# A one-core fp32 trunk layer: the first three up weight sets loaded into raw buffers of their own and split some blocks later, and the second part of the output projection reordered with its first two blocks interleaved

## The chip, the cores and the metric

The kernel runs on one core of one Trainium2 chip. The metric is the device time of one execution in microseconds (us). Before the change it is 1489.62 us, the median of three runs (1489.47 to 1491.08). A core has five engines that run their own instruction queues in order: PE (TensorE, matrix products), DVE (VectorE), ACT (ScalarE), POOL (GpSimd) and SP (SyncE, which here issues the weight transfers). In the profile, PEld is the weight load of PE.

## The reference

One layer for 320 tokens (256 of a prompt, 64 of a running sample), width 2048, in fp32:

```python
h = rmsnorm(x, g_pre_mix);  p = h @ w_in
a = conformer_conv(...)     # 8 channel groups of 128: GLU, causal depthwise conv of width 31,
                            # per-token group norm, silu
b = gated_delta(...)        # 8 heads of 128
x = x + rmsnorm(concat(a, b) @ w_out, g_post_mix)
h = rmsnorm(x, g_pre_ffn);  gu = causal_dwconv(h @ w_up)        # width 3, 2 x 5632 columns
x = x + rmsnorm((silu(gate) * up) @ w_down, g_post_ffn)
```

Beside the new x, the states of the convolutions and of the delta rule are returned.

## The kernel before

**Products.** All activations lie feature-major, as 16 blocks of 128 features by T = 320 tokens. A fp32 product is made of three products in a rounded type, fp32r: each weight and each activation is split into hi (rounded) and lo (the rest), and hi·hi, hi·lo and lo·hi are summed in one PSUM bank. So every 128x128 piece of a weight costs three matmuls of 128x320. A weight comes in pieces of 128 x 640, 768 or 1024: `load_dma` (L204-210) has SP load it into a ring `wst` of three buffers; `split_w` has ACT cast it to hi (L217) and DVE subtract to lo (L218), into a ring `wsp` of three pairs. `load_split` does both, under `boost`, a priority that lets the scheduler put them earlier than where they are written. Activations are split likewise, by `split_act` (L241 on ACT, L242 on DVE).

**Order.** The kernel is written in Python, and a scheduler orders the instructions by priority and data; `tc.issue_after(i)` forbids it to put the instructions inside ahead of i. Side work of the conv and delta heads is cut into jobs (`advance`) and into `taps`, which are handed out every few matmuls (`tick`); `finish` and `finish_conv` write what is left.

**Conv blocks.** The conv of one of the eight channel groups is 32 taps on DVE (L560 to L563, in two accumulators, added by L557). `conv_tail` then goes PE transposes `pt_c` (L578), DVE statistics (L580, L581, L584, L585), POOL (L586, L587), ACT normalises (L591), PE transposes back (L595), ACT silu (L597), and the split into `bh7`, `bl7` (for group 7). Groups 6 and 7 are the last ones: their taps run beside the first part of the output projection.

**Output projection, two parts.** `KORDER` lists the 16 feature blocks of concat(a, b) in the order of use, and `bx(k)` gives the pair of block KORDER[k]. In the first part (L1004 to L1009) 15 of the 16 output blocks n sum over the first K1 = 11 entries of KORDER; each takes two weight pieces (6 and 5 wide, matmuls L233, L234, then L237). `while jobs: advance(jobs[0])` then writes the rest of the conv jobs. In the second part (L1046 to L1072) all 16 output blocks take the last five entries, 5, 6, 7 (conv) and 14, 15 (delta): one piece `w_out2` of 128x640 each, three matmuls (L1061, L1062, L1063) for each entry, then the evacuation: DVE adds to the first part (L1069), ACT squares (L1032), DVE sums the squares (L1034), ACT scales by g2 (L1072). SP also loads block n of x into x1 (L1050).

**The up group.** A norm follows (`rstd`, `rstd_rows`, and `keep_warm`, L280, dummy matmuls), and a loop over the 16 feature blocks k on DVE and ACT: L1093 and L1094 (DVE, x1 + m·rb1), L1098 (ACT, hi2) and L1099 (DVE, lo2). `up_group` (L1108 to L1118) computes the first four output blocks of the up projection in four PSUM banks at once, k by k: 192 matmuls of L1117. Its weights are eight sets, each 128 x 4 x 256 of `w_up` (width 1024, two k's of four blocks), `upw[0]` to `upw[7]`. Two of them are loaded and split at n = 4 and 8 of the second part, through the ring `wst`, into a pool `ug` of two pairs; the six others in the norm loop, at k = 1, 3, ... 11, into the ring `wsp`. After that come the rest of the up projection and the down projection, which have no line in the diff.

Of the kernel before, what the change touches and what calls it, by code (L numbers as in the profile page):

```python
# [9 lines left out]
F32 = mybir.dt.float32  # L10
# [7 lines left out]
P = 128  # L18
D = 2048
KB = D // P  # L20
TP = 256
TS = 64
T = TP + TS
# [5 lines left out]
HALF = 1024  # L29
# [42 lines left out]
FIRST_V = 32  # L72
NFIRST = len(FIRST)
FW = NFIRST * P
KORDER = (0, 1, 2, 3, 4, 8, 9, 10, 11, 12, 13, 5, 6, 7, 14, 15)

S_ = 4

# [22 lines left out]
def trunk_kernel(ctx, tc, ins, outs):  # L101
    nc = tc.nc
    V, S, G, PE = nc.vector, nc.scalar, nc.gpsimd, nc.tensor
    PRI_W = 600
    boost = [0]
# [20 lines left out]
    def advance(job, behind=None):  # L126
        with tc.issue_after(behind or dense[0]), tc.high_priority(offset=PRI_J):
            try:
                wait, job[2], job[3], *kind = next(job[1])
                job[0] = dense[1] + wait  # L130
                job[4] = kind
            except StopIteration:
                jobs.remove(job)
        return next(i for i in reversed(nc.cur_bb.bb.instructions) if i.engine == dense[0].engine)
# [10 lines left out]
    def newest(engine, n0):  # L145
        return next((i for i in reversed(nc.cur_bb.bb.instructions[n0:]) if i.engine == engine), None)
# [32 lines left out]
    wst = ctx.enter_context(tc.tile_pool(name="wst", bufs=3))  # L179
# [3 lines left out]
    ps_p = ctx.enter_context(tc.tile_pool(name="ps_p", bufs=2, space=PSUM))  # L183
    ps_t = ctx.enter_context(tc.tile_pool(name="ps_t", bufs=2, space=PSUM))
# [7 lines left out]
    def pv(name, a=None, b=None):  # L192
        o, w = PAR[name]
        if a is None:
            return par[:, o:o + w]
        return par[:, o + a:o + (a + 1 if b is None else b)]
# [5 lines left out]
    pre = []  # L202
    ready = {}

    def load_dma(src):
        w = wst.tile([P, HALF], F32, tag="w", name="w")
        dst = w[:, 0:src.free_size()]
        if len(src.shape) == 3:
            dst = dst.rearrange("p (a f) -> p a f", a=src.shape[1])
        nc.sync.dma_start(dst, src)  # L210
        return w

    def split_w(w, width, pool=None):
        pool = pool or wsp
        hi = pool.tile([P, HALF], F32R, tag="whi", name="whi")
        lo = pool.tile([P, HALF], F32R, tag="wlo", name="wlo")
        S.copy(hi[:, 0:width], w[:, 0:width])  # L217
        V.tensor_tensor(lo[:, 0:width], w[:, 0:width], hi[:, 0:width].bitcast(F32), ALU.subtract)  # L218
        return hi, lo

    def load_split(src, width, pool=None):
        with tc.high_priority(offset=boost[0]):
            return split_w(load_dma(src), width, pool)

    def block_matmul(ps, src, rhs, nks, final=True, first=True):
        nk = sum(nks)
        k0 = 0
        for nk_part in nks:
            hi, lo = load_split(src[:, k0 * P:(k0 + nk_part) * P], nk_part * P)
            for j in range(nk_part):  # L230
                xh, xl = rhs(k0 + j)
                wh = hi[:, j * P:(j + 1) * P]
                tick(PE.matmul(ps, wh, xh, start=(first and k0 + j == 0), stop=False))  # L233
                tick(PE.matmul(ps, wh, xl, start=False, stop=False))  # L234
            for j in range(nk_part):
                xh, xl = rhs(k0 + j)
                tick(PE.matmul(ps, lo[:, j * P:(j + 1) * P], xh, start=False, stop=(final and k0 + j == nk - 1)))  # L237
            k0 += nk_part
# [77 lines left out]
    with tc.tile_pool(name="xp", bufs=1) as xp:  # L316
# [25 lines left out]
        with tc.high_priority(offset=PRI_E):  # L342
            keep_warm(psw, NWARM)

            last = {}
# [22 lines left out]
            for k in range(KB):  # L368
                x = xt[k // 4][:, k % 4, :]
# [15 lines left out]
        for i, b in enumerate(FIRST):  # L385
            pool = (ps_t, ps_g)[i // 2]
            ready[b] = pool.tile([P, 512], F32, tag=pool.name[-1], name="ps_first")
        for k0 in range(0, KB, 2):
            hi, lo = pre[k0 // 2]
            for ks in ((k0,), (k0 + 1,)) if k0 < 4 else ((k0, k0 + 1),):  # L390
                for wt in (hi, lo):
                    for k in ks:
                        for i, b in enumerate(FIRST):
                            ps = ready[b][:, 0:T]
                            o = (k - k0) * FW + i * P
                            w = wt[:, o:o + P]
                            xh, xl = hx(k)
# [606 lines left out]
    for n in range(KB - 1):  # L1004
        psm = ps_p.tile([P, 512], F32, tag="p", name="psm")
        block_matmul(psm[:, 0:T], ins["w_out1"][n], bx, (6, 5))
        m.append(act.tile([P, T], F32, tag=f"hl{n}", name=f"m{n}"))
        with tc.high_priority(offset=PRI_E):
            S.copy(m[n], psm[:, 0:T])  # L1009
    while jobs:  # L1010
        advance(jobs[0])
    pa.close()
    pb = ctx.enter_context(ExitStack())
    res = pb.enter_context(tc.tile_pool(name="res", bufs=1, reuse_waits="tile"))
    fb = pb.enter_context(tc.tile_pool(name="fb", bufs=2, reuse_waits="tile"))
    x1 = res.tile([P, KB, T], F32, tag="x1", name="x1")
# [17 lines left out]
            V.tensor_tensor(acc, acc, sq, ALU.add)  # L1034
        return sq

    ug = tc.tile_pool(name="ug", bufs=2, reuse_waits="tile")
    ugp = ug.__enter__()
    up_src = ins["w_up"][0:4].rearrange("a p f -> p a f")

    def up_weights(kk, pool=None):
        return load_split(up_src[:, :, kk * 256:(kk + 1) * 256], HALF, pool)

    upw = []
    nk2 = KB - K1
    for n in range(KB):  # L1046
        hi, lo = load_split(ins["w_out2"][n], nk2 * P)
        if n in (4, 8):
            upw.append(up_weights(len(upw), ugp))
        nc.sync.dma_start(x1[:, n:n + 1, :], ins["x"][:, n:n + 1, :])  # L1050
        if n == KB - 1:
            nc.sync.dma_start(fpar, ins["fpar"])
        whole = n == KB - 1
        pool = (ps_p, ps_t)[n // 2 % 2]
        psm = pool.tile([P, 512], F32, tag=pool.name[-1], name="psm2")
        if whole:
            block_matmul(psm[:, 0:T], ins["w_out1"][n], bx, (6, 5), False)
        for j in range(nk2):
            xh, xl = bx(K1 + j)
            o = j * P  # L1060
            PE.matmul(psm[:, 0:T], hi[:, o:o + P], xh, start=(j == 0 and not whole), stop=False)  # L1061
            PE.matmul(psm[:, 0:T], hi[:, o:o + P], xl, start=False, stop=False)  # L1062
            PE.matmul(psm[:, 0:T], lo[:, o:o + P], xh, start=False, stop=(j == nk2 - 1))  # L1063
        with tc.high_priority(offset=PRI_E):
            if whole:
                m.append(act.tile([P, T], F32, tag=f"hl{n}", name=f"m{n}"))
                src = psm[:, 0:T]
            else:
                V.tensor_tensor(m[n], m[n], psm[:, 0:T], ALU.add)  # L1069
                src = m[n]  # L1070
            last = square_acc(n, src)
            held = S.activation(m[n], src, AF.Identity, scale=pv("g2", n)).ins  # L1072
    boost[0] = 0
    rb2 = act.tile([P, T], F32, tag="rb", name="rb2")
    hi2, lo2 = [], []
    with tc.high_priority(offset=PRI_E):
        psw = ps_p.tile([P, 512], F32, tag="p", name="psw")
        rr, mm = rstd([acc, last])
        keep_warm(psw, 5, mm)
        rb1, mm = rstd_rows(rr)  # L1080
        keep_warm(psw, 10, mm)
        split = None
        for k in range(KB):
            if k % 2 == 1 and k < 13:
                with ExitStack() as e:
                    if k < 7:
                        e.enter_context(tc.issue_after(split))
                        e.enter_context(tc.issue_after(held))
                    upw.append(up_weights(len(upw)))
            with ExitStack() as e:  # L1090
                if 0 < k < 4:
                    e.enter_context(tc.issue_after(added))
                V.tensor_tensor(m[k], m[k], rb1, ALU.mult)  # L1093
            added = V.tensor_tensor(x1[:, k, :], x1[:, k, :], m[k], ALU.add).ins  # L1094
            g = pv("g3", k)
            hi2.append(act.tile([P, T], F32R, tag=f"hh{k}", name=f"hi2_{k}"))
            lo2.append(act.tile([P, T], F32R, tag=f"hl{k}", name=f"lo2_{k}"))
            S.activation(hi2[k], x1[:, k, :], AF.Identity, scale=g)  # L1098
            split = V.scalar_tensor_tensor(lo2[k], x1[:, k, :], g, hi2[k].bitcast(F32), ALU.mult, ALU.subtract).ins  # L1099
# [8 lines left out]
    def up_group():  # L1108
        pss = [ps_p.tile([P, 512], F32, tag="p", name="psu") for _ in range(2)]
        pss += [ps_t.tile([P, 512], F32, tag="t", name="psu") for _ in range(2)]  # L1110
        for k in range(KB):
            hi, lo = upw[k // 2]
            xh, xl = hx2(k)
            for n, (wt, x) in enumerate(((hi, xh), (lo, xh), (hi, xl))):
                for i in range(4):
                    o = i * 256 + k % 2 * P
                    PE.matmul(pss[i][:, 0:T], wt[:, o:o + P], x, start=(k == 0 and n == 0), stop=(k == KB - 1 and n == 2))  # L1117
        return {0: pss[0], NFB: pss[1], 1: pss[2], NFB + 1: pss[3]}  # L1118

    first = up_group()  # L1120
    ug.__exit__(None, None, None)
    yp = pb.enter_context(tc.tile_pool(name="yp", bufs=1, reuse_waits="tile"))
    y = yp.tile([P, KB, T], F32, tag="y", name="y")
# [200 lines left out]
```

## Time and profile before

| what | value |
|---|---|
| median of 3 runs | 1489.62 us (1489.47 to 1491.08) |
| the profiled execution | 1489.37 us, of which span 1487.6 us |
| granted TensorE clock | 1.00 in the mean |
| PE, PEld | 1478.6 us (99%), 1458.2 us (98%) |
| DVE, ACT, POOL | 996.6 us (67%), 730.8 us (49%), 230.5 us (15%) |
| DMA | 224.22 MB, mean 151 GB/s |

The page gives the profiled execution; its span starts with the first and ends with the last instruction, and 1.8 us of the execution lie outside. Times within the trace count from the start of the span. The first part of the output projection ends at about 490 us, the second part runs to 534 us, and the up group from 538.6 to 568.6 us. In a row of the timeline the columns are start, duration (of the whole group, where there is an xcount at the end), engine, line, operation, output<-input, shape, and in brackets the engine's idle time before it with what ended that. Where instructions of one kind follow each other on an engine, their starts lie closer together than their durations, since each begins before the one ahead has fully left; the difference of two starts is what one costs the queue.

### The profile page before, as it was taken

What the parts mean: (1) busy time and instruction counts of PE and PEld (TensorE: products, weight loads), DVE (VectorE), ACT (ScalarE), POOL (GpSimd) and SP (SyncE); (2) the same over time, 40 slices, a digit from 0 to 9 for tenths busy, and PEclk for the clock granted to TensorE, in tenths of its full rate; (3) what the DMA queues carried; (4) which work ended last, traced back from release to release, by engine and by line L of the source; (5) the groups of instructions that cost most, each with busy time, mean ns of one, the idle gap of its engine ahead of it and who ended that gap; (6) DMA issues with size and microseconds to landing.
All of it is one profiled execution on the core that took longest, in us unless ns stands there. A gap on an engine that the chain in (4) does not pass through costs nothing.

```text
span 1487.6 us, 27264 instructions
## 1 busy us (share of the span) xinstructions
PE 1478.6 (99%) x10610; PEld 1458.2 (98%) x10610; DVE 996.6 (67%) x1816; ACT 730.8 (49%) x1331; POOL 230.5 (15%) x390
## 2 busy tenths in 40 slices
PE   9999999999999999999999999999999999999998
PEld 8999999999999989999999999999999999999997
DVE  6779888888989678756336665545666545656554
ACT  7674556655454656544334444334444334444453
POOL 0111101021010000322002322002232001223101
PEclk9999999999999999999999999999999999999999
DMA  8435453544444734444554444554444455444453
GB/s 294 140 115 167 158 151 110 147 156 138 129 122 145 238 128 146 146 156 121 153 168 155 145 154 135 143 162 158 156 143 147 136 148 168 153 156 143 136 148 119
DMA packets 98281, 224.22 MB, mean 151 GB/s; under 512 B 18792, under 2 KB 39528, under 8 KB 98152
## 3 DMA queue, kind: packets, MB, share of 16 engines
q1 hardware_dynamic: 98008, 222.45, 47.8%
q8 instruction: 83, 1.36, 0.4%
q14 instruction: 46, 0.38, 0.1%
q10 hardware_dynamic: 144, 0.03, 0.0%
HBM read 215.33 MB, written 7.12 MB: 150 GB/s over the span
## 4 chain that ended last, share of the span: by engine, by line
PE 95%; ACT 2%; DVE 1%; issue 1%; DMA 0%; POOL 0%; DVEq 0%; ACTq 0%; POOLq 0%
PE psu L237 13%; PE psu L234 13%; PE psu L233 13%; PE psdn L233 7%; PE psdn L234 7%; PE psdn L237 7%; PE psq L233 3%; PE psq L234 3%; PE psq L237 3%; PE psm L237 2%; PE psm L233 2%; PE psm L234 2%; PE psu L1117 1%; PE psv L233 1%; PE psgate L233 1%; PE ps_first L398 1%
## 5 line engine op out<-in xcount | busy, mean ns | idle before, releaser
L217 ACT CAST whi<-w 128x1024 fp32r<-128x1024 f32 (+2 forms) x440 | 412.6, 940 | 488.5 <-PE psu L234 169.7
L218 DVE TENSOR_TENSOR wlo<-w,whi 128x1024 fp32r<-128x1024 f32 (+2 forms) x440 | 477.2, 1085 | 191.4 <-ACT whi L217 123.9
L233 PE MATMUL psu<-hi,whi 128*128 128x320 f32 x1344 | 397.0, 309 | 0.0
L234 PE MATMUL psu<-lo,whi 128*128 128x320 f32 x1344 | 396.9, 309 | 0.0
L234 PEld LDWEIGHTS psu<-lo,whi 128*128 128x128 f32 x1344 | 252.3, 188 | 0.0
L233 PEld LDWEIGHTS psu<-hi,whi 128*128 128x128 f32 x1344 | 252.2, 188 | 0.0
L237 PE MATMUL psu<-hi,wlo 128*128 128x320 f32 x1344 | 224.4, 309 | 0.0
L237 PEld LDWEIGHTS psu<-hi,wlo 128*128 128x128 f32 x1344 | 204.1, 188 | 0.0
L234 PE MATMUL psdn<-gl,whi 128*128 128x320 f32 x660 | 195.9, 310 | 0.0
L1150 POOL COPY nffn<-fbuf 128x2 f32<-128x2 f32 x88 | 99.5, 1131 | 586.7 <-DVE fbuf L1148 583.5
L1148 DVE TENSOR_TENSOR fbuf<-psu,rb 128x256 f32<-128x256 f32 x88 | 37.4, 424 | 169.1 <-PE psu L237 169.0
L233 PE MATMUL psdn<-gh,whi 128*128 128x320 f32 x480 | 142.8, 309 | 0.0
L234 PEld LDWEIGHTS psdn<-gl,whi 128*128 128x128 f32 x660 | 123.9, 188 | 0.3
L233 PE MATMUL psq<-hh,whi 128*128 128x320 f32 x352 | 106.0, 314 | 0.0
L234 PE MATMUL psq<-hl,whi 128*128 128x320 f32 x352 | 104.1, 309 | 0.0
L233 PEld LDWEIGHTS psdn<-gh,whi 128*128 128x128 f32 x480 | 90.1, 188 | 0.0
L237 PE MATMUL psdn<-gh,wlo 128*128 128x320 f32 x480 | 89.9, 309 | 0.0
L237 PEld LDWEIGHTS psdn<-gh,wlo 128*128 128x128 f32 x480 | 75.3, 188 | 0.0
L233 PEld LDWEIGHTS psq<-hh,whi 128*128 128x128 f32 x352 | 66.1, 188 | 0.4
L234 PEld LDWEIGHTS psq<-hl,whi 128*128 128x128 f32 x352 | 66.1, 188 | 0.2
L563 DVE SCALAR_TENSOR_TENSOR cvt<-ub,par,cvt 128x320 f32<-128x320 f32 x120 | 65.3, 545 | 0.1
L1193 DVE TENSOR_TENSOR y<-y,psdn 128x320 f32<-128x320 f32 x45 | 22.0, 488 | 58.7 <-PE psdn L237 58.7
(356 smaller groups left out, 2485.2 us busy)
## 6 DMA issues: line engine op xcount, KB each, us to landing
w<-in_w_up SPq DMA_DIRECT2D x176, 512.0 KB
w<-in_w_in SPq DMA_DIRECT2D x88, 512.0 KB
w<-in_w_down SPq DMA_DIRECT2D x64, 384.0 KB
w<-in_w_down SPq DMA_DIRECT2D x64, 320.0 KB
w<-in_w_out SPq DMA_DIRECT2D x32, 320.0 KB
w<-in_w_out SPq DMA_DIRECT2D x16, 384.0 KB
w<-in_w_first SPq DMA_DIRECT2D x6, 512.0 KB
wtp<-wsp SPq DMA_DIRECT2D x4, 640.0 KB
```

Of the source, the lines that this page charges most:

```text
L217: S.copy(hi[:, 0:width], w[:, 0:width])
L218: V.tensor_tensor(lo[:, 0:width], w[:, 0:width], hi[:, 0:width].bitcast(F32), ALU.subtract)
L233: tick(PE.matmul(ps, wh, xh, start=(first and k0 + j == 0), stop=False))
L234: tick(PE.matmul(ps, wh, xl, start=False, stop=False))
L237: tick(PE.matmul(ps, lo[:, j * P:(j + 1) * P], xh, start=False, stop=(final and k0 + j == nk - 1)))
L398: tick(PE.matmul(ps, w, xh, start=(k == 0 and wt is hi), stop=(k == KB - 1 and wt is lo)))
L563: return lambda: V.scalar_tensor_tensor(acc, x, w, acc, ALU.mult, ALU.add)
L1117: PE.matmul(pss[i][:, 0:T], wt[:, o:o + P], x, start=(k == 0 and n == 0), stop=(k == KB - 1 and n == 2))
L1148: V.tensor_tensor(buf[:, 2:258], psu[:, 0:TP], rb2[:, 0:TP], ALU.mult)
L1150: G.tensor_copy(nffn[:, b, 0, :], buf[:, 256:258])
L1193: V.tensor_tensor(y[:, n, :], y[:, n, :], psd[:, 0:T], ALU.add)
```

## The change

1. `KORDER` ends in 5, 14, 15, 6, 7 instead of 5, 6, 7, 14, 15, so in the second part the two delta blocks are used ahead of conv groups 6 and 7.
2. Blocks 0 and 1 of the second part are interleaved: four entries of block 0, four of block 1, then the last entry (conv 7) of block 0 and of block 1, and only then both evacuations.
3. `load_dma` can load into another pool. The first three up weight sets go into a pool `ur` of two raw buffers, loaded at n = 3, 6, 10 (`up_load`) and split at n = 6, 10, 14 (`up_split`) into `ug`, now three pairs. The norm loop makes five sets (k = 3, 5, ... 11).
4. The load and split of `w_out2` for n = 2 may not stand ahead of `flush`, the newest ACT instruction of the jobs' rest.

```diff
-KORDER = (0, 1, 2, 3, 4, 8, 9, 10, 11, 12, 13, 5, 6, 7, 14, 15)
+KORDER = (0, 1, 2, 3, 4, 8, 9, 10, 11, 12, 13, 5, 14, 15, 6, 7)
...
+    flush = len(nc.cur_bb.bb.instructions)
     while jobs:
         advance(jobs[0])
+    flush = newest(mybir.EngineType.Activation, flush)
...
-    ug = tc.tile_pool(name="ug", bufs=2, reuse_waits="tile")
+    ug = tc.tile_pool(name="ug", bufs=3, reuse_waits="tile")
     ugp = ug.__enter__()
+    ur = tc.tile_pool(name="ur", bufs=2, reuse_waits="tile")
+    urp = ur.__enter__()
     up_src = ins["w_up"][0:4].rearrange("a p f -> p a f")
-    def up_weights(kk, pool=None):
-        return load_split(up_src[:, :, kk * 256:(kk + 1) * 256], HALF, pool)
+    def up_load(kk, pool=None):
+        with tc.high_priority(offset=boost[0]):
+            return load_dma(up_src[:, :, kk * 256:(kk + 1) * 256], pool)
+    def up_split(w, pool=None):
+        with tc.high_priority(offset=boost[0]):
+            return split_w(w, HALF, pool)
...
     for n in range(KB):
-        hi, lo = load_split(ins["w_out2"][n], nk2 * P)
-        if n in (4, 8):
-            upw.append(up_weights(len(upw), ugp))
+        with ExitStack() as e:
+            if n == 2:
+                e.enter_context(tc.issue_after(flush))
+            w2 = load_split(ins["w_out2"][n], nk2 * P)
+        if n in (3, 6, 10):
+            upr.append(up_load(len(upr), urp))
+        if n in (6, 10, 14):
+            upw.append(up_split(upr[len(upw)], ugp))
...
+        if n == 0:
+            opened[0] = psm, w2
+            second(n, psm[:, 0:T], w2, range(nk2 - 1))
+            continue
+        if n == 1:
+            second(n, psm[:, 0:T], w2, range(nk2 - 1))
+            second(0, opened[0][0][:, 0:T], opened[0][1], (nk2 - 1,))
+            second(n, psm[:, 0:T], w2, (nk2 - 1,))
+        else:
+            second(n, psm[:, 0:T], w2, range(nk2))
...
-            if k % 2 == 1 and k < 13:
+            if k % 2 == 1 and 1 < k < 13:
...
-                    upw.append(up_weights(len(upw)))
+                    upw.append(up_split(up_load(len(upw))))
```

`second` holds the three matmuls and `evacuate` the evacuation, both as before.

What the scheduler makes of it is seen in the order of the instructions. In the rows below `w` is a raw weight piece, `whi` and `wlo` its parts, and a number behind a name tells tiles of one name apart.

On SP, in the first part of the output projection, before:

```order
L210 DMA w_5924<-in_w_out1 128x640
L210 DMA w_5956<-in_w_out1 128x768
L210 DMA w_5984<-in_w_out1 128x640
L210 DMA w_6012<-in_w_out1 128x768
L210 DMA w_6040<-in_w_out1 128x640
```

and after:

```order
L210 DMA w_5924<-in_w_out1 128x640
L210 DMA w_6406<-in_w_up 128x4x256
L210 DMA w_6492<-in_w_up 128x4x256
L210 DMA w_5956<-in_w_out1 128x768
L210 DMA w_5984<-in_w_out1 128x640
L210 DMA w_6610<-in_w_up 128x4x256
L210 DMA w_6012<-in_w_out1 128x768
```

The three loads of up sets stand in the first part, although they are written at n = 3, 6 and 10 of the second; there, none is left.

On DVE at the same place, where conv 6 gets its last sum (`cvt_4967`) and the taps of conv 7 (`cvt_5305`, `odd_5306`) begin, before:

```order
L218 TENSOR_TENSOR wlo_5903<-w_5900,whi_5902 128x768
L557 TENSOR_TENSOR cvt_4967<-cvt_4967,odd_4968 128x320
L563 SCALAR_TENSOR_TENSOR cvt_5305<-ub1_588,par_81,cvt_5305 128x320
L562 TENSOR_SCALAR odd_5306<-ub1_588,par_81 128x320
L563 SCALAR_TENSOR_TENSOR cvt_5305<-ub1_588,par_81,cvt_5305 128x320
L563 SCALAR_TENSOR_TENSOR odd_5306<-ub1_588,par_81,odd_5306 128x320
L218 TENSOR_TENSOR wlo_5927<-w_5924,whi_5926 128x640
L242 TENSOR_TENSOR bl5_5842<-af_5839,bh5_5841 128x320
```

and after:

```order
L218 TENSOR_TENSOR wlo_5903<-w_5900,whi_5902 128x768
L557 TENSOR_TENSOR cvt_4967<-cvt_4967,odd_4968 128x320
L218 TENSOR_TENSOR wlo_6495<-w_6406,whi_6494 128x1024
L218 TENSOR_TENSOR wlo_6613<-w_6492,whi_6612 128x1024
L218 TENSOR_TENSOR wlo_5927<-w_5924,whi_5926 128x640
L242 TENSOR_TENSOR bl5_5842<-af_5839,bh5_5841 128x320
L562 TENSOR_SCALAR odd_5306<-ub1_588,par_81 128x320
L563 SCALAR_TENSOR_TENSOR cvt_5305<-ub1_588,par_81,cvt_5305 128x320
L580 BN_STATS bst_5876<-pt_c_5875 128x6 x2
```

The splits of up sets 0 and 1 stand ahead of nearly all taps of conv 7; that of set 2 (`wlo_6729`) follows ten rows on, still ahead of most of them.

On DVE at the end of conv 7, before:

```order
L563 SCALAR_TENSOR_TENSOR cvt_5305<-ub1_588,par_81,cvt_5305 128x320
L218 TENSOR_TENSOR wlo_6152<-w_6149,whi_6151 128x640
L557 TENSOR_TENSOR cvt_5305<-cvt_5305,odd_5306 128x320
L242 TENSOR_TENSOR bl6_6107<-af_6104,bh6_6106 128x320
L218 TENSOR_TENSOR wlo_6194<-w_6191,whi_6193 128x768
L218 TENSOR_TENSOR wlo_6222<-w_6219,whi_6221 128x640
L580 BN_STATS bst_6166<-pt_c_6165 128x6 x2
```

and after:

```order
L242 TENSOR_TENSOR bl6_6107<-af_6104,bh6_6106 128x320
L563 SCALAR_TENSOR_TENSOR cvt_5305<-ub1_588,par_81,cvt_5305 128x320
L218 TENSOR_TENSOR wlo_6194<-w_6191,whi_6193 128x768
L563 SCALAR_TENSOR_TENSOR odd_5306<-ub1_588,par_81,odd_5306 128x320
L563 SCALAR_TENSOR_TENSOR cvt_5305<-ub1_588,par_81,cvt_5305 128x320
L563 SCALAR_TENSOR_TENSOR odd_5306<-ub1_588,par_81,odd_5306 128x320
L218 TENSOR_TENSOR wlo_6222<-w_6219,whi_6221 128x640
L563 SCALAR_TENSOR_TENSOR cvt_5305<-ub1_588,par_81,cvt_5305 128x320
L557 TENSOR_TENSOR cvt_5305<-cvt_5305,odd_5306 128x320
L580 BN_STATS bst_6166<-pt_c_6165 128x6 x2
```

The last sum of conv 7 (L557) stands behind `bl6_6107`, `wlo_6194` and `wlo_6222`, which stood behind it before. On PE the transposes that read it, before:

```order
L234 MATMUL psm_6124<-bl13_4881,whi_6151 128x320
L578 MATMUL pt_c_6165<-cst_82,cvt_5305 128x128 x3
L237 MATMUL psm_6124<-bp0_3030,wlo_6152 128x320
L237 MATMUL psm_6124<-bp1_3695,wlo_6152 128x320 x2
L237 MATMUL psm_6124<-bp2_4871,wlo_6152 128x320 x2
```

and after:

```order
L234 MATMUL psm_6124<-bl13_4881,whi_6151 128x320
L237 MATMUL psm_6124<-bp0_3030,wlo_6152 128x320
L237 MATMUL psm_6124<-bp1_3695,wlo_6152 128x320 x2
L237 MATMUL psm_6124<-bp2_4871,wlo_6152 128x320
L578 MATMUL pt_c_6165<-cst_82,cvt_5305 128x128 x3
L237 MATMUL psm_6124<-bp2_4871,wlo_6152 128x320
```

PE takes them four matmuls later in its own order than before. At the start of the second part, PE before takes conv 7 (`bh7`) behind nine matmuls, blocks 0 and 1 mixed by the scheduler; after, behind twelve of block 0 and twelve of block 1.

More of the change, by code (lines that the diff above doesn't have):

```diff
@@ L203, in trunk_kernel, with load_dma @@
     ready = {}
-    def load_dma(src):
-        w = wst.tile([P, HALF], F32, tag="w", name="w")
+    def load_dma(src, pool=None):
+        w = (pool or wst).tile([P, HALF], F32, tag="w", name="w")
         dst = w[:, 0:src.free_size()]
@@ L1035, in square_acc, with second, evacuate @@
         return sq
-    ug = tc.tile_pool(name="ug", bufs=2, reuse_waits="tile")
+    ug = tc.tile_pool(name="ug", bufs=3, reuse_waits="tile")
     ugp = ug.__enter__()
+    ur = tc.tile_pool(name="ur", bufs=2, reuse_waits="tile")
+    urp = ur.__enter__()
     up_src = ins["w_up"][0:4].rearrange("a p f -> p a f")
-    def up_weights(kk, pool=None):
-        return load_split(up_src[:, :, kk * 256:(kk + 1) * 256], HALF, pool)
-    upw = []
-    nk2 = KB - K1
-    for n in range(KB):
-        hi, lo = load_split(ins["w_out2"][n], nk2 * P)
-        if n in (4, 8):
-            upw.append(up_weights(len(upw), ugp))
[L1050 to L1058, printed above, removed]
+    def up_load(kk, pool=None):
[4 more added lines that the diff above has]
+            return split_w(w, HALF, pool)
+    upw, upr = [], []
+    nk2 = KB - K1
+    def second(n, psm, w, js):
+        hi, lo = w
+        for j in js:
             xh, xl = bx(K1 + j)
             o = j * P
-            PE.matmul(psm[:, 0:T], hi[:, o:o + P], xh, start=(j == 0 and not whole), stop=False)
-            PE.matmul(psm[:, 0:T], hi[:, o:o + P], xl, start=False, stop=False)
-            PE.matmul(psm[:, 0:T], lo[:, o:o + P], xh, start=False, stop=(j == nk2 - 1))
+            PE.matmul(psm, hi[:, o:o + P], xh, start=(j == 0 and n < KB - 1), stop=False)
+            PE.matmul(psm, hi[:, o:o + P], xl, start=False, stop=False)
+            PE.matmul(psm, lo[:, o:o + P], xh, start=False, stop=(j == nk2 - 1))
+    last = held = None
+    def evacuate(n, psm, whole):
+        nonlocal last, held
         with tc.high_priority(offset=PRI_E):
@@ L1072, in trunk_kernel @@
             held = S.activation(m[n], src, AF.Identity, scale=pv("g2", n)).ins
+    opened = {}
+    for n in range(KB):
+        with ExitStack() as e:
[6 more added lines that the diff above has]
+            upw.append(up_split(upr[len(upw)], ugp))
+        nc.sync.dma_start(x1[:, n:n + 1, :], ins["x"][:, n:n + 1, :])
+        if n == KB - 1:
+            nc.sync.dma_start(fpar, ins["fpar"])
+        whole = n == KB - 1
+        pool = (ps_p, ps_t)[n // 2 % 2]
+        psm = pool.tile([P, 512], F32, tag=pool.name[-1], name="psm2")
+        if whole:
+            block_matmul(psm[:, 0:T], ins["w_out1"][n], bx, (6, 5), False)
+        if n == 0:
[8 more added lines that the diff above has]
+            second(n, psm[:, 0:T], w2, range(nk2))
+        for n, psm in ((0, opened[0][0]), (1, psm)) if n == 1 else ((n, psm),):
+            evacuate(n, psm, whole)
     boost[0] = 0
@@ L1120, in trunk_kernel @@
     first = up_group()
+    ur.__exit__(None, None, None)
     ug.__exit__(None, None, None)
```

## The prediction

> **What bounds the kernel now.** I read the page first (engines, clock, the chain), then PE's list of waits, then a table of stretches around the change, and last the rows of each place.
>
> ```profile
> PE 1478.6 (99%) x10610; PEld 1458.2 (98%) x10610; DVE 996.6 (67%) x1816; ACT 730.8 (49%) x1331; POOL 230.5 (15%) x390
> PE 95%; ACT 2%; DVE 1%; issue 1%; DMA 0%; POOL 0%; DVEq 0%; ACTq 0%; POOLq 0%
> PE psm L1063 <- DVE wlo L218: 1.1, 2, 0.8
> core 0: us, PE busy (x) PEld busy (x) DVE busy (x) ACT busy (x) POOL busy (x), PEclk, DMA share, GB/s
> 452.00:478.00 26.00, 26.00 (x181) 25.97 (x181) 24.45 (x53) 12.25 (x22) 2.09 (x2) 1.00 0.46 137
> 494.00:511.00 17.00, 17.00 (x118) 16.90 (x116) 12.50 (x21) 13.19 (x23) 0.00 (x0) 1.00 0.88 287
> 511.00:515.00 4.00, 2.89 (x18) 2.45 (x17) 2.44 (x5) 1.83 (x4) 0.00 (x0) 1.00 0.80 231
> 538.60:568.60 30.00, 29.70 (x195) 28.43 (x194) 29.43 (x56) 15.24 (x25) 0.00 (x0) 1.00 0.38 122
> ```
>
> PE is busy for 99% of the span and is 95% of the chain that ended last: time falls only where PE stalls, and work moved to another engine costs only where PE comes to wait for it. The change adds and removes no matmul, cast or subtraction; it moves up splits. So I look for stalls that go and stalls that come. The stretches differ. In the first part (452 to 478) PE is full but DVE has only 1.55 us free in 26. In the second part DVE has 4.50 of 17 free, but the transfers are at 0.88 and 287 GB/s, and right behind PE loses time (511 to 515). In the up group DVE is full again, 29.43 of 30.
>
> **Part 1, the start of the second part (gain 0.31).**
>
> ```profile
> 491.76 0.31 PE L1063 MATMUL psm<-bh,wlo 128*128 128x320 f32 x1
> 492.81 0.31 PE L1063 MATMUL psm<-bh,wlo 128*128 128x320 f32 x1
> 510.86 0.31 PE L1062 MATMUL psm<-bl,whi 128*128 128x320 f32 x1
> 511.98 0.41 PE L1063 MATMUL psm<-bh,wlo 128*128 128x320 f32 x1 [0.81 <-DVE wlo L218]
> 512.23 0.31 PE L1061 MATMUL psm<-bh,whi 128*128 128x320 f32 x1
> 514.15 0.31 PE L1062 MATMUL psm<-bl,whi 128*128 128x320 f32 x1
> 514.76 0.42 PE L1063 MATMUL psm<-bh,wlo 128*128 128x320 f32 x1 [0.30 <-DVE wlo L218]
> 515.01 0.31 PE L1061 MATMUL psm<-bh,whi 128*128 128x320 f32 x1
> 539.56 0.75 PE L1117 MATMUL psu<-hi,wlo 128*128 128x320 f32 x4
> ```
>
> Unhindered, a matmul costs 0.147: in the last row four of them take 0.75, one 0.31, so three steps are 0.44. From 491.76 to 492.81 five starts take 1.05 instead of 0.73: 0.31 lost where conv 7 is first read. Now 24 matmuls, 3.5 us, stand ahead of that read instead of nine, 1.3; that is 2.2 more cover for a stall of 0.31. So it goes: 0.31 (bounds 0 and 0.31). The interleave itself costs nothing: the same matmuls, and two PSUM banks for blocks 0 and 1 as before.
>
> **Part 2, the jam in the middle of the second part (gain 1.65).** By the rows above, 510.86 to 512.23 is 1.37 for two steps worth 0.29, a loss of 1.08; 514.15 to 515.01 is 0.86, a loss of 0.57; together 1.65. What stands behind them:
>
> ```profile
> 508.48 1.73 ACT L217 CAST whi<-w 128x1024 fp32r<-128x1024 f32 x2 [1.70 <-DMA w<-in_w_up]
> 506.61 6.44 DMA w<-in_w_out
> w<-in_w_up SPq DMA_DIRECT2D x176, 512.0 KB
> ```
>
> ACT waited 1.70 for an up set, and the w_out piece for the second stall took 6.44 to land (the row of the chain). The change takes two loads of 512 KB, 1.05 MB, out of a stretch that moves 17 x 287 kB = 4.9 MB, and also two casts and two splits of 1024. Both stalls lose their cause, so I take all of 1.65; bounds 0 (the transfers stay late anyway) and 1.65.
>
> **Part 3, the up group (gain 1.1).**
>
> ```profile
> 538.61 1.12 PE L1117 MATMUL psu<-hi,whi 128*128 128x320 f32 x4
> 568.62 0.31 PE L234 MATMUL psu<-lo,whi 128*128 128x320 f32 x1
> 539.56 1.22 DVE L218 TENSOR_TENSOR wlo<-w,whi 128x1024 fp32r<-128x1024 f32 x1
> 540.69 0.54 DVE L1099 SCALAR_TENSOR_TENSOR lo<-x,par,hi 128x320 fp32r<-128x320 f32 x1
> ```
>
> 192 matmuls at 0.147 are 28.2; the group takes 568.62 - 538.61 = 30.01. Of the 1.8 over, up to 0.4 is three other matmuls in the stretch (195 against 192). The first 0.36 (538.61 to 539.56, 0.95 for four matmuls instead of 0.59) comes ahead of any split and stays. So 1.05 to 1.45 can go. DVE is full here, so PE goes at its pace, and one split fewer (five, not six) takes 540.69 - 539.56 = 1.13 out of its queue. I take 1.1; bounds 0 (the last splits, not their sum, set the end) and 1.45.
>
> **Part 4, what the moved splits hold up (cost 3.25).** By the order, the three up splits now run on DVE in the first part, ahead of the taps of conv 7.
>
> ```profile
> 453.04 0.48 DVE L557 TENSOR_TENSOR cvt<-cvt,odd 128x320 f32<-128x320 f32 x1
> 464.29 0.96 DVE L218 TENSOR_TENSOR wlo<-w,whi 128x768 fp32r<-128x768 f32 x1 [1.55 <-ACT whi L217]
> 477.44 0.49 DVE L557 TENSOR_TENSOR cvt<-cvt,odd 128x320 f32<-128x320 f32 x1
> 477.84 0.49 DVE L242 TENSOR_TENSOR bl<-af,bh 128x320 fp32r<-128x320 f32 x1
> 478.24 1.69 DVE L218 TENSOR_TENSOR wlo<-w,whi 128x768 fp32r<-128x768 f32 x2
> 479.51 0.49 PE L578 MATMUL pt_c<-cst,cvt 128*128 128x128 f32 x3
> 479.76 0.98 PE L237 MATMUL psm<-bp,wlo 128*128 128x320 f32 x5
> 462.37 1.16 ACT L591 ACTIVATE un<-pt_c,gnm,grs 128x128 f32<-128x128 f32 x3 [3.98 <-POOL gnm L587]
> ```
>
> Conv 7's last sum (L557) began at 477.44 and ended at 477.93; PE took its transposes (L578) at 479.51, so 1.6 us of slack. Now three splits of 1.14 stand ahead, 3.42 us, and by the order also `bl6` (0.40, 477.84 to 478.24) and two w_out splits (1.60 of the 1.69 row, less the overlap): 2.00. L557 begins at 477.44 + 5.42 = 482.86 and ends at 483.35. PE's turn comes four matmuls later than before, 479.51 + 0.59 = 480.10. PE stands for 483.35 - 480.10 = 3.25 us, with everything behind it in its queue: the fifth L237, then blocks n of the first part.
>
> Can DVE's idle 1.55 ahead of 464.29 take some of it up? It waits there for a cast behind conv 6's `un` (462.37), which waits for POOL, which waits for DVE's statistics. Those are pushed less than the taps: six taps that stood ahead of them now stand behind. But the rows between statistics and that cast are the same four taps and one split, so the idle time moves along and is not used: 0 taken up, 1.55 at most. The casts can wait for their loads:
>
> ```profile
> 445.20 2.58 SPq L210 DMA_DIRECT2D w<-in_w_out  x2
> 452.22 0.73 ACT L217 CAST whi<-w 128x640 fp32r<-128x640 f32 x1 [1.33 <-issue]
> 458.35 0.31 PE L233 MATMUL psm<-bp,whi 128*128 128x320 f32 x1
> ```
>
> The up loads are issued behind the second of these, at 447.78. 1.05 MB at 287 GB/s land at 451.4, at 137 GB/s at 455.4; with a cast of 0.87 set 1 is ready at 452.3 or 456.3, and DVE wants it at 453.52 + 1.14 = 454.66. So 0 to 1.6 more; I take 0, since the queue's load (0.46) leaves room. Bounds of the term: 1.7 and 4.9. The w_out cast at 452.22, first read by PE at 458.35, comes behind two up casts (1.74): with set 1 as late as 455.4 it ends at 455.4 + 0.87 + 0.73 = 457.0, still ahead of its reader, so nothing there. The slots for casts cost nothing else: ACT is free for 13.75 of 26. SP's later w_out loads stand behind three more issues; what times them is the ring of three buffers, that is the pace of the splits, not SP.
>
> The `flush` rule holds one w_out2 load until the jobs' last ACT work is placed; two pieces for blocks 0 and 1 (24 matmuls) cover it, so nothing.
>
> **Sum.** -0.31 - 1.65 - 1.1 + 3.25 = +0.19 on this execution's 1489.37, that is 1489.6. The median is 0.25 above that execution: 1489.8. I say 1489.7. With every bound the kind way (-0.31 - 1.65 - 1.45 + 1.7) it is 1.7 faster, the other way 4.9 slower.
>
> **The clock, row and rule.** A pause of 3.1 us (3.25 less the 0.16 for which the matmul ahead still runs) is longer than any that this trace has (its longest wait inside is 0.81), and a new question is whether the granted clock, 1.00 throughout, holds.
>
> ```profile
> 1.42 3.59 PE L280 MATMUL psw<-wz 128*128 128x512 bf16 x8 [1.42 <-POOL wz L250]
> 5.54 0.47 PE L398 MATMUL ps_first<-hh,whi 128*128 128x320 f32 x1
> 5.81 0.47 PE L400 MATMUL ps_first<-hl,whi 128*128 128x320 f32 x1
> 6.82 0.31 PE L400 MATMUL ps_first<-hl,whi 128*128 128x320 f32 x1
> ```
>
> After the start PE runs at 0.27 a matmul (5.54 to 5.81, each 0.47 long) and at 6.82 has the 0.31 of all later ones: 5.4 us from 1.42 at 0.147 / 0.27 = 0.55 of the pace, a loss of 2.4. That is what a drop would cost. The Trainium skill, "TensorE: Matmul & The Clock Gate", section "Why this matters for your kernels", asks for no PE-idle gaps over about 3 us, since one idle window halves the clock, and its Part 1 gives a free-running window of about 3.4 us. By it a pause of 3.1 lies at the limit and is an estimate away from it on either side: under it the sum stays 1489.7, over it 2.4 come on top. No run here shows it, and its limit is in none of the sums here.
>
> **Rivals.**
> - Clock drop (slower). Up set 1 lands 1.6 late (137 GB/s), PE stands 4.9 instead of 3.25, and the clock falls: 1489.7 + 1.6 + 2.4 = 1493.7. It decides if a drop comes at all, from some pause between 0.81 and 4.9; a shorter pause with a drop gives 1492.1. For it: the start shows that the clock is low after standing. Against: transfers have room.
> - Late landing without a drop: 1491.3.
> - The jam stays: x1 and w_out2 alone still fill the queue, part 2 brings nothing, 1491.3. Against: 4.9 - 1.05 = 3.9 MB in 17 us is 226 GB/s, under the 287 that were reached.
> - Conv 7 isn't late (the change does only what it says): the idle 1.55 and more is used up, or the splits wait aside; parts 1 to 3 alone, -3.06, 1486.6.
>
> **Chances.** A measurement of this kernel can tell about 0.2%, 2.98 us: below 1486.6 is faster, above 1492.6 slower. My forecast 0.63 (its own range, with some idle time used or half a us of late landing, 1488.2 to 1491.0); jam 0.09; late landing 0.08; clock drop 0.11; conv 7 not late 0.09. Faster: most of the last, 0.08. Slower: most of the drop and a little of late landing with the jam, 0.12. Same: 0.80. The range leaves out the two outer cases: 1487.4 to 1492.5.
>
> **What would show it.** Right: at L578 of conv 7 a PE wait for DVE's L557 of 3 us; three 1024 splits on DVE between 453 and 462; no PE wait at L1063 in the second part, and the stretch of 17 us well under 287 GB/s; an up group of 28.9 instead of 30.0. Wrong: no wait at L578 (part 4 falls, 1486.6); a matmul step of 0.27 behind it (clock); waits at L1063 as before (part 2 falls).

## The result, and the profile after

The changed kernel takes 1491.63 us (median of 22 runs, 1490.35 to 1492.94) against 1489.62 (22 runs, 1488.54 to 1491.08) of the kernel before beside it: 1.0013 of its time, 95% interval 1.0007 to 1.0019. That is 2.0 us slower, inside the range of 1487.4 to 1492.5, and 1.9 above the forecast of 1489.7. The profiled execution has a span of 1489.4 us against 1487.6.

From PE's list of waits of the changed kernel (us in all, times, longest):

```profile
PE pt_c L578 <- DVE cvt L557: 3.3, 1, 3.3
```

The same kernel by stretches, with the columns of the table of before:

```profile
452.00:478.00 26.00, 26.00 (x180) 25.75 (x179) 24.39 (x48) 14.81 (x25) 1.62 (x2) 1.00 0.57 171
478.00:490.00 12.00, 8.70 (x52) 8.44 (x51) 8.41 (x21) 3.94 (x8) 1.05 (x2) 0.86 0.39 115
497.00:514.00 17.00, 17.00 (x118) 17.00 (x117) 12.79 (x24) 12.40 (x24) 0.00 (x0) 1.00 0.86 277
514.00:518.00 4.00, 4.00 (x29) 4.00 (x29) 2.79 (x5) 2.51 (x5) 0.45 (x2) 1.00 0.79 283
```

One wait is new, 3.3 us at the transposes of conv 7, and the waits at L1063 are gone from the list. The stretch from 478 to 490 has lost 3.30 us of PE and has a granted clock of 0.86. In the middle of the second part PE is now full (514 to 518: 4.00 of 4, before 2.89). The stretch before it still moves 277 GB/s.

PE at the new wait, the columns as in the timelines above:

```profile
479.61 0.75 PE L237 MATMUL psm<-bp,wlo 128*128 128x320 f32 x4
483.66 0.90 PE L578 MATMUL pt_c<-cst,cvt 128*128 128x128 f32 x3 [3.30 <-DVE cvt L557]
484.21 0.61 PE L237 MATMUL psm<-bp,wlo 128*128 128x320 f32 x1
484.62 0.47 PE L233 MATMUL psm<-bh,whi 128*128 128x320 f32 x1
484.89 0.47 PE L234 MATMUL psm<-bl,whi 128*128 128x320 f32 x1
486.49 0.32 PE L234 MATMUL psm<-bl,whi 128*128 128x320 f32 x1
486.65 0.31 PE L233 MATMUL psm<-bh,whi 128*128 128x320 f32 x1
```

The same place by stretches; the granted clock is the third number from the end:

```profile
480.20:483.70 3.50, 0.20 (x3) 0.04 (x1) 3.37 (x7) 0.83 (x1) 0.00 (x0) 0.91 0.34 95
483.70:486.60 2.90, 2.90 (x12) 2.90 (x13) 1.90 (x9) 0.42 (x1) 0.00 (x0) 0.52 0.35 111
484.00:486.00 2.00, 2.00 (x10) 2.00 (x9) 1.40 (x6) 0.42 (x1) 0.00 (x0) 0.50 0.37 137
486.60:490.00 3.40, 3.40 (x25) 3.40 (x24) 0.94 (x3) 1.95 (x5) 1.05 (x2) 1.00 0.30 96
```

The turn was 479.61 + 4 x 0.147 = 480.20, the start is 483.66: 3.46 lost. Then the step from one matmul to the next is 0.27 (484.62 to 484.89), as at the start of the kernel, until 486.5, and 0.15 from there. By the stretches the granted clock is 0.50 in the middle of the drop (484 to 486), 0.52 in the mean from 483.7 to 486.6, and 1.00 behind. At a clock of 0.50, the means of 0.91 over 3.50 us and 0.52 over 2.90 make 0.63 and 2.78 us of low clock. So the drop lasted 3.4 us, and its first 0.6 lay in the pause. Three transposes and eight matmuls took 2.83 (483.66 to 486.49). At full pace they take 1.43 by the rows of before (0.25, from 479.51 to 479.76, and 8 x 0.147), or 1.56 by those of the run with dummies below (three transposes and five matmuls in 1.12 from 483.99 to 485.11, three more at 0.147). So 1.3 to 1.4 us are lost to the clock.

ACT's timeline ahead of that, at the cast of up set 1:

```profile
453.98 1.05 ACT L217 CAST whi<-w 128x1024 fp32r<-128x1024 f32 x1 [1.10 <-DMA w<-in_w_up]
```

DVE's timeline: the splits of the three up sets (the second row here holds that of set 1 and a w_out split), its idle time behind conv 6, and conv 7's last sum:

```profile
453.31 1.23 DVE L218 TENSOR_TENSOR wlo<-w,whi 128x1024 fp32r<-128x1024 f32 x1
455.07 1.96 DVE L218 TENSOR_TENSOR wlo<-w,whi 128x1024 fp32r<-128x1024 f32 x2 [0.53 <-ACT whi L217]
460.03 1.23 DVE L218 TENSOR_TENSOR wlo<-w,whi 128x1024 fp32r<-128x1024 f32 x1
465.06 0.96 DVE L218 TENSOR_TENSOR wlo<-w,whi 128x768 fp32r<-128x768 f32 x1 [1.08 <-ACT whi L217]
483.11 0.49 DVE L557 TENSOR_TENSOR cvt<-cvt,odd 128x320 f32<-128x320 f32 x1
```

PE's timeline at the start of the up group and at the first matmul behind it:

```profile
541.40 1.11 PE L1153 MATMUL psu<-hi,whi 128*128 128x320 f32 x4
570.31 0.31 PE L233 MATMUL psu<-hi,whi 128*128 128x320 f32 x1
```

Conv 7's last sum began at 483.11 (477.44 before), and the up group takes 28.91 instead of 30.01. But the two ends are not the same matmul: the row of before at 568.62 (L234) is the second of the block behind the group, that of after at 570.31 (L233) the first. In before, the first had run inside the group, by PE's timeline of before:

```profile
563.19 0.31 PE L233 MATMUL psu<-hi,whi 128*128 128x320 f32 x1
```

So 0.15 of the 1.10 is a matmul that changed its place, and 0.95 is gained. What PE and its weight loads waited for in the group before (L1117), and below it what ACT's L1098 there waited for (us in all, times):

```profile
ACT hi L1098: 1.1, 3
DVE x L1094: 13.1, 10
```

### The profile page after: what moved, and what is told of

The parts are those of the page before. It is cut to its first block, busy times and chain, and to the rows that moved or that the text cites. A ratio compares the mean times of both kernels' runs of the same rounds, so it can differ in the third digit from the quotient of the medians.

```text
span 1489.4 us, 27262 instructions
## 1 busy us (share of the span) xinstructions
PE 1478.3 (99%) x10610; PEld 1458.8 (98%) x10610; DVE 997.5 (67%) x1816; ACT 730.2 (49%) x1331; POOL 229.2 (15%) x390
## 4 chain that ended last, share of the span: by engine, by line
PE 94%; DVE 2%; ACT 1%; issue 1%; DMA 1%; POOL 0%; SPq 0%; DVEq 0%; ACTq 0%
PE psu L237 13%; PE psu L234 13%; PE psu L233 13%; PE psdn L233 7%; PE psdn L234 7%; PE psdn L237 7%; PE psq L233 3%; PE psq L234 3%; PE psq L237 3%; PE psu L1153 2%; PE psv L233 1%; PE psgate L233 1%; PE psgate L237 1%; PE psv L237 1%; PE psgate L234 1%; PE psv L234 1%
## 5 line engine op out<-in xcount | busy, mean ns | idle before, releaser
L233 PE MATMUL psu<-hi,whi 128*128 128x320 f32 x1344 | 397.1, 309 | 0.0
L234 PE MATMUL psu<-lo,whi 128*128 128x320 f32 x1344 | 396.9, 309 | 0.0
L234 PEld LDWEIGHTS psu<-lo,whi 128*128 128x128 f32 x1344 | 252.3, 188 | 0.0
L233 PEld LDWEIGHTS psu<-hi,whi 128*128 128x128 f32 x1344 | 252.3, 188 | 0.0
L234 PE MATMUL psdn<-gl,whi 128*128 128x320 f32 x660 | 195.9, 310 | 0.0
L233 PE MATMUL psdn<-gh,whi 128*128 128x320 f32 x480 | 142.8, 309 | 0.0
L234 PEld LDWEIGHTS psdn<-gl,whi 128*128 128x128 f32 x660 | 123.9, 188 | 0.3
L233 PE MATMUL psq<-hh,whi 128*128 128x320 f32 x352 | 106.0, 314 | 0.0
L234 PE MATMUL psq<-hl,whi 128*128 128x320 f32 x352 | 104.1, 309 | 0.0
L233 PEld LDWEIGHTS psdn<-gh,whi 128*128 128x128 f32 x480 | 90.1, 188 | 0.0
L233 PEld LDWEIGHTS psq<-hh,whi 128*128 128x128 f32 x352 | 66.1, 188 | 0.4
L234 PEld LDWEIGHTS psq<-hl,whi 128*128 128x128 f32 x352 | 66.1, 188 | 0.2
```

## The experiments

My theory after the result: the three up splits on DVE make conv 7's last sum late, PE stands for it, and standing costs a second time through the clock; the gains came nearly as forecast. All kernels below are the changed kernel with the edit shown. Each group ran beside the kernel before: 1488.98 us (33 runs) for the first four, 1488.59 (31) for the next four, 1488.62 (15) for the last; ratios are to that kernel's runs.

| run | edit | median us | ratio (95%) | PE idle at conv 7's transposes |
|---|---|---|---|---|
| e1_hold | no up split ahead of conv 7's last ACT work | 1486.43 | 0.9984 (0.9975 to 0.9993) | none |
| e5_hold3 | the same, three raw buffers | 1486.52 | 0.9984 (0.9975 to 0.9993) | none |
| e4_hold_loads | splits and loads held | 1489.49 | 1.0004 (0.9995 to 1.0012) | none |
| e2_warm | 16 dummy matmuls in the pause | 1490.74 | 1.0010 (1.0001 to 1.0019) | 0.41 behind them |
| e6_one | one split early, two held | 1486.09 | 0.9979 (0.9969 to 0.9988) | none |
| e7_two | two early, one held | 1490.72 | 1.0009 (1.0000 to 1.0019) | 2.5 |
| e8_longer | three early, more DVE work | 1492.20 | 1.0019 (1.0010 to 1.0029) | 3.4 |
| e3_order | only the order of blocks | 1489.57 | 1.0004 (0.9995 to 1.0014) | none |
| e9_pause | one early, more DVE work | 1487.56 | 0.9993 (0.9984 to 1.0002) | 0.8 |

**Splits held.**

```diff
-            upw.append(up_split(upr[len(upw)], ugp))
+            with tc.issue_after(flush):
+                upw.append(up_split(upr[len(upw)], ugp))
```

> The changed kernel, with the three up splits forbidden to stand ahead of the last ACT work of conv 7; the loads of sets 0 and 1 stay in the first part, that of set 2 comes in the second. My theory (the three splits on DVE hold up the taps of conv 7; PE waits 3.3 us at L578, and its clock falls behind the pause, 1.4 us): the wait and the slow steps go, the gains stay, so 1491.6 - 3.5 - 1.4 = 1486.8, with up to 0.6 given back where splits meet the second part. Rival (the early transfers and casts, not the splits, make conv 7 late): a wait of 1 us or more stays at L578, 1488 or above. Rival (the slow steps have nothing to do with the pause): they stay, 1488.2.

Measured 1486.43, span 1484.6: 4.8 under the changed kernel's span, and the trace's two losses, 3.46 and 1.3 to 1.4, make 4.8 to 4.9. PE's timeline at the transposes:

```profile
479.52 0.49 PE L578 MATMUL pt_c<-cst,cvt 128*128 128x128 f32 x3
```

DVE's timeline at conv 7's last sum:

```profile
477.45 0.48 DVE L557 TENSOR_TENSOR cvt<-cvt,odd 128x320 f32<-128x320 f32 x1
```

A stretch of the second part, where the splits now run:

```profile
495.00:520.00 25.00, 25.00 (x172) 24.93 (x171) 21.21 (x38) 20.75 (x39) 1.44 (x4) 1.00 0.88 283
```

Transposes and sum stand where they stood before, to 0.01 us, although sets 0 and 1 are still loaded in the first part: it was the splits, not the transfers. (The edit holds ACT's casts together with DVE's subtractions; that DVE's part did it is read from the changed kernel's trace, where DVE is busy for 3.37 of the 3.50 us from 480.20 to 483.70 and ACT for 0.83.) In the second part PE is full and DVE busy for 21.21 of 25. No wait at L1063, and nothing given back.

**Three raw buffers** (`ur` with `bufs=3`, splits held as above), so that the load of set 2 is early as well.

> As the run with held splits, but three raw buffers, so that all three up loads are in the first part. If transfers in the second part cost PE anything: 0 to 0.6 us faster than the run with held splits, 1486.4 to 1486.8. If three early loads push the first part's weights: a wait of PE in the first part that the run with held splits does not have, 1487 or above.

1486.52, the same span of 1484.6: one up load in the second part costs nothing, three in the first neither.

**Loads held too.**

```diff
+            with tc.issue_after(newest(mybir.EngineType.SP, 0)):
                 upr.append(up_load(len(upr), urp))
```

> As the run with held splits, but the three up loads too stand in the second part, each behind the w_out2 load of its n. My theory (the jam of the second part comes from up loads between w_out2 loads): PE waits at L1063 again, 1.0 to 1.7 us, so 1487.8 to 1488.5. Rival (the jam came from the old order of blocks or from splits on DVE): no such wait, 1486.8 as with held splits.

1489.49, 3.1 more than with held splits alone, and more than I expected (1487.8 to 1488.5). From PE's list of waits:

```profile
PE psm L1063 <- DVE wlo L218: 1.3, 2, 0.8
PE psm L1061 <- ACT whi L217: 0.4, 1, 0.4
PE pst L259 <- DVE acc L1036: 0.5, 2, 0.3
```

The same stretch as in the run with held splits:

```profile
495.00:520.00 25.00, 23.34 (x156) 22.55 (x155) 18.85 (x33) 18.23 (x33) 0.73 (x4) 1.00 0.86 274
```

The jam is back with loads in raw buffers of their own, so it does not come from sharing the ring `wst`; it comes from up loads standing between w_out2 loads. The bytes per second do not tell the two runs apart: 283 without waits, 274 with them. By which path the loads hold up PE differs from stall to stall. Ahead of the longest one here (0.76 at 517.47), ACT stood at the cast of an up set whose load was late, and the w_out2 cast came behind it without a wait of its own:

```profile
513.97 1.05 ACT L217 CAST whi<-w 128x1024 fp32r<-128x1024 f32 x1 [1.03 <-DMA w<-in_w_up]
515.39 0.71 ACT L217 CAST whi<-w 128x640 fp32r<-128x640 f32 x1
```

Before, the first stall was of this kind (ACT's row at 508.48, 1.70 for an up set), and at the second a w_out2 piece itself was late (6.44). No run parts the two paths.

**The pause filled.** In `conv_tail`, ahead of conv 7's transposes:

```diff
+        if b == 7:
+            pw = ps_g.tile([P, 512], F32, tag="g", name="pw")
+            keep_warm(pw, 16)
```

> The changed kernel with 16 dummy matmuls of 128x512 ahead of conv 7's transposes, some 3.5 us of PE work that depends on nothing; the transposes then stand ahead of all five L237 instead of behind four, which costs 0.6. My theory (the steps of 0.27 behind the pause are the clock after standing): L578 still at 483.7, the steps behind it 0.147, 1491.6 - 1.4 + 0.6 = 1490.8. Rival (they are slow for another reason, the restart itself or weights that come late): steps of 0.27 stay, 1492.2.

1490.74, expected 1490.8. PE's timeline:

```profile
479.95 3.63 PE L280 MATMUL pw<-wz 128*128 128x512 bf16 x16
483.99 0.55 PE L581 MATMUL pt_c<-cst,cvt 128*128 128x128 f32 x3 [0.41 <-DVE cvt L557]
484.29 0.98 PE L237 MATMUL psm<-bp,wlo 128*128 128x320 f32 x5
485.11 0.31 PE L233 MATMUL psm<-bh,whi 128*128 128x320 f32 x1
485.25 0.31 PE L234 MATMUL psm<-bl,whi 128*128 128x320 f32 x1
```

The stretch behind the dummies:

```profile
483.90:487.00 3.10, 3.01 (x21) 3.01 (x22) 2.11 (x10) 0.43 (x1) 0.17 (x1) 1.00 0.32 106
```

The transposes come no earlier (483.99), and everything behind them runs at 0.147 with a clock of 1.00. So the slow steps are the clock's answer to standing, not the restart.

**One and two splits early.** As the first edit, with `issue_after(flush)` only from set 1 or set 2 on (`if len(upw) >= 1`, `>= 2`).

> The changed kernel with only up set 0 split in the first part, sets 1 and 2 held as in the run with held splits. My theory (the wait grows with the work that stands ahead of conv 7's last sum): 1.14 + 0.40 (bl6) later, so the sum ends at 477.93 + 1.54 = 479.5, and PE's turn is 479.5: a wait of 0 to 0.5 us, no drop of the clock, 1486.4 to 1486.9. Rival (any up split in the first part costs PE its length): 1.1 or more, 1487.5.

> The changed kernel with up sets 0 and 1 split in the first part, set 2 held. My theory: 2.28 + 0.40 + 0.87 later, and 0.5 for the late load of set 1, so the sum ends at 481.98 against PE's turn at 479.5: a wait of 2.0 to 2.5 us. If a pause of that length leaves the clock alone: 1486.4 + 2.4 = 1488.8, steps of 0.147 behind it. If it drops as behind 3.3: 1490.2, steps of 0.27.

One split early: 1486.09, 0.3 below what was expected, and no wait; the sum (L557) ends at 477.99 + 0.49 = 478.48 and PE's turn is 478.91. (This trace runs 0.62 earlier throughout, 452.42 against 453.04 at conv 6's sum: beside that, PE's turn is where it was and the sum 1.2 later.) Two: 1490.72, a wait of 2.5 as expected, and the clock dropped; that is 0.5 above the 1490.2 expected for a drop. The run with one split, DVE's timeline and then PE's:

```profile
452.42 0.49 DVE L557 TENSOR_TENSOR cvt<-cvt,odd 128x320 f32<-128x320 f32 x1
477.99 0.49 DVE L557 TENSOR_TENSOR cvt<-cvt,odd 128x320 f32<-128x320 f32 x1
```

```profile
478.91 0.49 PE L578 MATMUL pt_c<-cst,cvt 128*128 128x128 f32 x3
```

The run with two, PE's timeline:

```profile
482.54 0.55 PE L578 MATMUL pt_c<-cst,cvt 128*128 128x128 f32 x3 [2.52 <-DVE cvt L557]
482.84 1.05 PE L237 MATMUL psm<-bp,wlo 128*128 128x320 f32 x5
483.69 0.47 PE L233 MATMUL psm<-bh,whi 128*128 128x320 f32 x1
483.96 0.47 PE L234 MATMUL psm<-bl,whi 128*128 128x320 f32 x1
486.89 0.95 PE L237 MATMUL psm<-bh,wlo 128*128 128x320 f32 x5
```

and its stretches:

```profile
482.60:483.50 0.90, 0.90 (x7) 0.90 (x8) 0.90 (x3) 0.00 (x0) 0.00 (x0) 1.00 0.68 250
483.50:487.00 3.50, 3.50 (x16) 3.50 (x15) 1.76 (x8) 0.82 (x3) 1.04 (x2) 0.52 0.60 174
```

With two, PE resumes at 482.54 and runs at full pace for 0.9; only then, from 483.5 to 487.0, is the clock 0.52. So the loss comes behind work that had already started: the twelve matmuls from 483.69 to 486.89 took 3.20 instead of 1.76, 1.44 lost. The wait does not grow by a split's length: none, one, two, three early splits give 0, 0, 2.5 and 3.3, since slack takes up the first and the w_out splits that the scheduler puts ahead of the sum come on top.

**A longer pause.** Four operations on DVE that leave the values as they are, ahead of the last sum of group 7 alone:

```diff
+                        for _ in range(4):
+                            V.tensor_scalar(odd, odd, 1.0, None, ALU.mult)
                         V.tensor_tensor(cvt, cvt, odd, ALU.add)
```

> The changed kernel with four extra DVE operations (odd times 1) ahead of conv 7's last sum, and one w_out split more ahead of it by the order; 2.7 us later on DVE, while PE's turn comes 2.3 later than in the changed kernel. My theory: a wait of 3.3 + 0.4 to 4.2 us and a drop of the clock behind it that costs 1.4 to 2.4; 1491.6 + 0.5 to 2 = 1492.1 to 1493.6. Rival (the drop in the changed kernel was an accident of that place): steps of 0.147 behind the wait, 1491 or less.

1492.20, at the low end of what was expected; the pause of 3.43 is shorter than the 3.7 to 4.2 expected, and the clock dropped again. PE's timeline:

```profile
485.34 0.89 PE L584 MATMUL pt_c<-cst,cvt 128*128 128x128 f32 x3 [3.43 <-DVE cvt L561]
```

The stretch behind it:

```profile
485.40:488.90 3.50, 3.50 (x15) 3.50 (x16) 1.75 (x7) 0.00 (x0) 0.00 (x0) 0.51 0.28 94
```

**A shorter pause**: the run with one early split and two such operations.

> The kernel with one early split (1486.1, no wait of PE at conv 7) with two extra DVE operations (odd times 1) ahead of conv 7's last sum, and by the order one w_out split more ahead of it: 0.92 + 0.87 later, less 0.43 of slack, so PE stands 1.2 to 1.4 us at the transposes. If the clock drops behind any pause over a threshold that lies under 1.2: steps of 0.27, 1486.1 + 1.4 + 1.6 = 1489.1 in most runs. If the threshold lies between 1.3 and 2.5: steps of 0.147, clock 1.000 in all runs, 1487.4 to 1487.6.

1487.56; the pause came out shorter than I meant, by PE's timeline:

```profile
481.39 0.55 PE L584 MATMUL pt_c<-cst,cvt 128*128 128x128 f32 x3 [0.83 <-DVE cvt L561]
482.50 0.31 PE L233 MATMUL psm<-bh,whi 128*128 128x320 f32 x1
482.65 0.31 PE L234 MATMUL psm<-bl,whi 128*128 128x320 f32 x1
```

Full pace behind 0.83. The limit lies somewhere between 0.83 and 2.52; no run narrows it further.

**Only the order of blocks**: `KORDER`, interleave and the flush rule, with the up sets as before.

> Only the new KORDER, the interleave and the flush rule; up sets as before (two in the second part, six in the norm loop). My theory: the small losses at the first read of conv 7 go (0.3), the waits at L1063 in the middle of the second part stay at 1 to 1.7, the up group stays at 30.0: 0.3 faster than before, which the time alone can't tell. Rival (the order of blocks made the jam): no wait at L1063, 2 faster.

1489.57, no gain in time (the span of this trace is 1488.0 against 1487.6). The small losses at the first read of conv 7 are gone from the trace, but PE's list of waits still has the jam, and it is longer than before (1.1, 2 times):

```profile
PE psm L1063 <- DVE wlo L218: 1.6, 3, 0.9
```

So the order of blocks took away the 0.3 and alone made the jam worse; that the jam is gone is the work of the moved loads. Why the new order lengthens it was not tested.

## Why the prediction was right, and what it missed

- **Part 1** (0.31): right. The losses at 492 are gone, with the order alone as with the whole change; the time of the order alone does not show it, since the jam grew.
- **Part 2** (1.65): right in size; no wait at L1063 is left. The reason needs a correction. I argued from the bytes (287 GB/s, 226 without the up loads); the stretch still moves 277, and runs with and without waits move 274 and 283. What counts is that no late up load stands in the way, be it between w_out2 loads on SP or with its cast ahead of theirs on ACT. One in the second part did no harm (e1_hold), three did (e4_hold_loads, waits of 1.7 in all), and two cost 1.1 with the old order and 1.6 with the new (e3_order), so the number alone does not set the price. One row was misread as well: the x2 at 508.48 holds one cast of an up set and one of a w_out2 piece, so 0.87 is not what a cast of an up set takes (1.05 in the row at 453.98); nothing in the sum hangs on that.
- **Part 3** (1.1): right in mechanism, 0.95 in size. The 30.01 - 28.91 = 1.10 agree by luck, since 0.15 of them is the matmul at 563.19. DVE's queue set the pace of the up group: PE waited for ACT's L1098, and that for DVE's L1094.
- **Part 4** (3.25): right in mechanism, measured 3.46. Of the two things that I set to zero both came: set 1's cast waited for its load (1.10 on ACT, 0.53 on DVE), and part of DVE's idle time was used (1.55 became 1.08). They cancel to 0.06; the sum began 0.25 later than worked out, and the other 0.19 was not followed up.
- **The clock**: here the forecast failed. I made the sum with the clock at 1.00 behind a pause of 3.1 and put the drop into a rival that needed late landing and a pause of 4.9. It came behind 3.30, at 1.3 to 1.4 and not 2.4: I had taken the whole slow start as the price, 5.4 us, while the drop here lasts 3.4 us, of which PE stood for the first 0.6. The line "a shorter pause with a drop gives 1492.1" is the one that names what happened (1491.63).
- **The range**: it held in part by luck. 1491.63 lies above the forecast's own range (1488.2 to 1491.0), to which I gave 0.63. It is inside 1487.4 to 1492.5 because that left room for a late landing and for a jam that stays (1491.3 each), and neither is what happened; the clock is.

On the spans: -0.31 - 1.65 - 0.95 + 3.46 + 1.3 to 1.4 = +1.85 to +1.95, and 1489.4 - 1487.6 = +1.8. The Trainium skill, "TensorE: Matmul & The Clock Gate", section "Why this matters for your kernels", was the better guide with its gap of about 3 us than my sum; but a gap of 2.52 dropped the clock too, so the measured limit here is lower.

## What to carry to other kernels

Work that is moved to an earlier stage has to be placed on the engine that is free there: DVE was 24.45 of 26 busy in the first part and 21.21 of 25 with the splits in the second, and the same splits cost 4.8 us in the one and nothing in the other. A high priority finds the earliest place, not the free one; an order rule for one line of code made 1.0013 of the time into 0.9984. And where PE is the bound, waits of 2.52 and 3.30 us cost 1.3 to 1.4 us more through the clock, so such a wait is worth more than it shows in the list of waits.

## What the runs showed of the hardware

- The granted clock falls to half behind PE pauses of 2.52, 3.30 and 3.43 us, and stays at 1.00 behind 0.83. The three drops all last 3.4 us, though the pauses differ: at a clock of 0.50, the 0.52 over 3.50 us behind the pause of 2.52 makes 3.36, the 0.51 over 3.50 behind that of 3.43 makes 3.43, and the changed kernel's two stretches make 0.63 + 2.78 = 3.41. What it costs is what PE loses while it works at that clock, 1.3 to 1.4 us where 0.6 of the drop lay in the pause, and 1.44 for twelve matmuls in e7_two, where none did.
- The drop need not begin where PE resumes. In the changed kernel it began 0.6 us ahead of that; behind the pause of 2.52 PE ran at full pace for 0.9 us first. So the length of the pause is not all that decides; no run here moves the start of one pause. A list of waits shows none of it; the granted clock of short stretches does.
- It may not fall in every execution. A drop of 3.4 us at half the clock takes 1.7 of 1489 us, 0.0011, off the mean clock, so an execution listed with 1.000 had none. Of ten runs with the pause of 2.5, two took 1488.69 and 1488.93 with a mean clock of 1.000, eight 1490.08 to 1491.04 with 0.998 or 0.999. The run with the longer pause has one such (1489.53, its lowest), the changed kernel one of 22 (1490.70). Only one execution of each kernel has a trace, so whether PE stood as long in these is not known, and the kernel before scatters by as much (1487.45 to 1491.09): this stays a reading and is not shown.
